# The first head's values' product made to wait for both heads' copies, in the causal attentions and the MLA of a two-block transformer

## The chip, the cores and the metric

The kernel runs on one core of a Trainium2 chip. The metric is the device time of one execution in microseconds (us). Before the change it is 3457.11 us, the median of three runs (3451.3 to 3459.18).

## The reference

Two layers of a hybrid block (a causal attention with forget gates called fox, a sparse attention called nsa, and an MLP) are followed by two layers of a second block (MLA with gated linear attention, then grouped attention, each with a mixture of 16 experts). All is float32, for 512 tokens of width 1024. The change touches the attentions below. With 512 tokens the selection of nsa keeps every block and its window covers every earlier token, so its selected and window branches are plain causal attentions as well.

```python
# fox: 8 heads of 64; nsa's selected and window branches: 8 heads of 64 over 2 key heads
s = jnp.einsum('bhqd,bhkd->bhqk', qi, k) * scale
s = s + ci[..., :, None] - c[..., None, :]            # fox alone
s = jnp.where(kpos[None, :] <= qpos[:, None], s, -jnp.inf)
p = jax.nn.softmax(s, axis=-1)
o = jnp.einsum('bhqk,bhkd->bhqd', p, v)
# MLA: 8 heads, no mask
s = (jnp.einsum('bqhd,bkhd->bhqk', qn, k_nope)
     + jnp.einsum('bqhd,bkd->bhqk', qp, k_pe)) * scale
pr = jax.nn.softmax(s, axis=-1)
o = jnp.einsum('bhqk,bkhd->bqhd', pr, v)
```

## The kernel before

Tokens are held feature-major: 128 features on the partitions, 512 tokens along the free axis. A large product is split in three (`mm3`, L234 to L236): the high part of the weights by the high and the low part of the input, and the low part of the weights by the high part, each a 128x512 product. The weights are split by a cast on ScalarE (L225) and a subtraction (L228).

The causal attentions take two heads at a time. `causal_scores` (L605 to L612) makes for one head four query blocks of 128, with 128, 256, 384 and 512 keys: products into a buffer `s`, a row maximum on VectorE (L610), an exponential on ScalarE (L612). `causal_pv` (L617 to L639) then scales both heads' rows (L288, called from it), and for each key block k of four:

- the probabilities of head 0 are transposed on TensorE into a buffer `pt` (L629, 4 - k transpositions), and VectorE copies them to `PT` (L635);
- the same for head 1, copied by ScalarE (L633);
- one product for each head (L638) multiplies the values `V[h][k]` (128 keys by 64 columns) by `PT[h]` (128 keys by 512, 384, 256 or 128 queries) and adds it to `o`. Head 0's result stands on partitions 0 to 63 of `o`, head 1's on 64 to 127, so each product uses 64 of the 128 columns of TensorE's array.

There are two buffers `pt`, four `PT` and two `s`. `causal_pv` is called 12 times in a layer: four times by fox and eight by nsa (two key heads, two branches, two pairs of heads), so 24 times, with 192 value products.

MLA calls `full_pair` (L997 to L1036) four times. It works on 256 queries at a time, transposes two key blocks at once for each head (L1024), copies head 0 on VectorE (L1030) and head 1 on ScalarE (L1028), and makes four value products of 128x256 (L1035): head 0 and 1 of one key block, then of the next. That is 16 groups of four.

A scheduler sets the order of instructions on every engine when the program is built: it runs a simulated timeline and gives each engine an instruction that its simulation holds to be ready. So products of other work (the projections of the next heads in fox, the merge of fox's output in nsa, handed in piece by piece by generators) stand on TensorE between an attention's steps. Each engine then runs its instructions in that order, and waits where an operand isn't there. No order written by hand holds in these stages; the mixtures of experts have one (`weave`, `keep_order`). In the expert products (L1725) two experts share the array in the same way, 64 columns each, and are written alternately.

Of the kernel before, what the change touches and what calls it, by code (L numbers as in the profile page):

```python
# [147 lines left out]
class K:  # L148
# [303 lines left out]
    def fox(self, l, at, pp, w, XH, XL, v, cneg, B, comp):  # L452
# [3 lines left out]
        def project(pr):  # L456
            if pr % 2 == 0:
                ws[0] = [self.wcols(w, c + 128 * pr) for c in (0, 512)]
            wq, wk = [x[:, :, (pr % 2) * 128:(pr % 2) * 128 + 128] for x in ws[0]]
            Q = self.q_stack(at, pp, wq, XH, XL, None)  # L460
            zk = self.k_proj(at, pp, wk, XH, XL)
            KH = at.tile([128, 2, T], F32R, name="KH", bufs=2)
            KL = at.tile([128, T], F32R, name="KL", bufs=2)
            for h in range(2):
                own = slice(64 * h, 64 * h + 64)
                oth = slice(64 - 64 * h, 128 - 64 * h)
                nc.scalar.copy(KH[own, h], zk[own])
                nc.scalar.copy(KH[oth, h], zk[own])
                nc.vector.tensor_sub(KL[own], zk[own], KH[own, h])
            parts[pr] = Q, KH, KL  # L470
# [25 lines left out]
        for pr in range(4):  # L496
            attend(pr)
            if pr < 2:
                project(pr + 2)

    def put_split(self, B, k, ps):
        self.nc.scalar.copy(B[0][k], ps)
        self.nc.vector.tensor_sub(B[1][k], ps, B[0][k])
# [113 lines left out]
    def causal_pv(self, at, pp, o, P, cf, V, first, last):  # L617

        nc, C = self.nc, self.C
        for h in range(2):  # L620
            for i in range(4):
                self.scale_rows(P[h][0][i], cf[h][:, i:i + 1])
        for k in range(4):
            n = 512 - 128 * k
            PT = []
            for h in range(2):
                ps = pp.tile([128, T], F32, name="pt", tag="t")
                for i in range(k, 4):
                    nc.tensor.transpose(ps[:, (i - k) * 128:(i - k + 1) * 128],  # L629
                                        P[h][0][i][:, k * 128:(k + 1) * 128], C["ident"])  # L630
                pt = at.tile([128, T], F32, name="PT", bufs=4)
                if h:
                    nc.scalar.copy(pt[:, :n], ps[:, :n])  # L633
                else:
                    nc.vector.tensor_copy(pt[:, :n], ps[:, :n])  # L635
                PT.append(pt)
            for h in range(2):
                nc.tensor.matmul(o[64 * h:64 * h + 64, 128 * k:], V[h][k], PT[h][:, :n],  # L638
                                 start=first and k == 0, stop=last and k == 3)  # L639

    def nsa(self, l, p, at, pp, w, XH, XL, gate, gcmp, B, KC, VC, fill):
        nc, tc, I, C, rB = self.nc, self.tc, self.ins, self.C, self.rB
# [354 lines left out]
    def full_pair(self, at, pp, o, passes, V):  # L997

        nc, C = self.nc, self.C
        for half in range(2):  # L1000
            P = []
            for h in range(2):
                p_ = at.tile([128, 2, T], F32, name="P", bufs=3)
                sums = at.tile([128, 2], F32, name="sums", bufs=4)
                mx = at.tile([128, 2], F32, name="mx", bufs=4)
                for i in range(2):
                    qs = slice(256 * half + 128 * i, 256 * half + 128 * i + 128)
                    s = pp.tile([128, T], F32, name="s", tag="s")
                    for j, (q, k) in enumerate(passes[h]):
                        nc.tensor.matmul(s, q[:, qs], k, start=j == 0, stop=j == len(passes[h]) - 1)  # L1010
                    nc.vector.tensor_reduce(mx[:, i:i + 1], s, axis=X, op=OP.max, negate=True)
                    nc.scalar.activation(p_[:, i], s, AF.Exp, bias=mx[:, i:i + 1], accum_out=sums[:, i:i + 1])
                nc.vector.reciprocal(sums, sums)
                for i in range(2):
                    self.scale_rows(p_[:, i], sums[:, i:i + 1])
                P.append(p_)
            for kp in range(2):
                PT = []
                for h in range(2):
                    ps = pp.tile([128, 2, 2, 128], F32, name="pt", tag="t")  # L1020
                    for kk in range(2):
                        for i in range(2):
                            k = 2 * kp + kk
                            nc.tensor.transpose(ps[:, kk, i], P[h][:, i, k * 128:(k + 1) * 128], C["ident"])  # L1024
                    pt = at.tile([128, 2, 256], F32, name="PT", bufs=4)
                    pv = ps.rearrange("p k i q -> p k (i q)")
                    if h:
                        nc.scalar.copy(pt, pv)  # L1028
                    else:
                        nc.vector.tensor_copy(pt, pv)  # L1030
                    PT.append(pt)
                for kk in range(2):
                    k = 2 * kp + kk
                    for h in range(2):
                        nc.tensor.matmul(o[64 * h:64 * h + 64, 256 * half:256 * half + 256], V[h][k], PT[h][:, kk],  # L1035
                                         start=k == 0, stop=k == 3)  # L1036

    def weave(self, plan, **chains):

# [1007 lines left out]
```

## Time and profile before

| | |
|---|---|
| median of three runs | 3457.11 us |
| the profiled execution's own time | 3446.95 us |
| its span | 3445.2 us |
| TensorE busy (PE) | 3255.6 us, 94% of the span |
| VectorE (DVE), ScalarE (ACT), GpSimd (POOL) busy | 1553.8, 1051.8, 581.3 us |
| mean granted TensorE clock | 0.978 of full speed |

The profile is one execution. PE is TensorE's matmuls, PEld its weight loads. A matmul of full float32 operands (L638, L1035, L1725) appears as two records, a transposition and an `mm3` product as one, so "x2" in a row of L638 is one value product. The end of a matmul is modelled and lies after the moment at which the next may start; what an instruction costs is read from the start of one to the start of the next.

### The profile page before, as it was taken

The numbers are of one execution on the slowest core, as the hardware profiler recorded it, in microseconds if no ns is written. First come the engines' busy times: TensorE is split into PE (matmuls) and PEld (weight loads), VectorE is DVE, ScalarE is ACT, GpSimd is POOL, SyncE is SP. The second block draws the span as 40 slices with busy tenths as digits, with TensorE's granted clock in tenths as the row PEclk, the third lists the DMA queues.
The fourth block names the chain that finished last, engine by engine and source line by source line (L and its number), as shares of the span: only waits on it lengthen the run. The fifth ranks groups of instructions, "written<-read, shape, count | busy, mean of one in ns | idle before, by whom it ended". The sixth has DMA issues, their size and how long they took to land. (4 is left out here: it accounts for less than half of the span.)

```text
span 3445.2 us, 37016 instructions
## 1 busy us (share of the span) xinstructions
PE 3255.6 (94%) x14746; PEld 2111.6 (61%) x14746; DVE 1553.8 (45%) x2435; ACT 1051.8 (31%) x1856; POOL 581.3 (17%) x437
## 2 busy tenths in 40 slices
PE   8999999999999999999998889999998889999997
PEld 5666678888766666888875676434345547444343
DVE  6555464334655545444458755122124666211214
ACT  3333333223344333322246423111113443111011
POOL 2012121001101111200121224000002552200001
PEclk9999999999999999999999989999999999999998
DMA  5101132224310111233321115999994113999997
GB/s 186 50 25 50 49 99 86 94 92 136 98 49 25 49 49 63 96 98 98 98 71 39 50 60 205 421 421 396 420 421 178 37 38 122 372 421 395 421 421 296
DMA packets 223724, 585.07 MB, mean 170 GB/s; under 512 B 17600, under 2 KB 160320, under 8 KB 173376
## 3 DMA queue, kind: packets, MB, share of 16 engines
q1 hardware_dynamic: 223120, 581.92, 44.6%
q8 instruction: 116, 1.90, 0.2%
q10 hardware_dynamic: 432, 0.79, 0.1%
q14 instruction: 56, 0.46, 0.0%
HBM read 580.57 MB, written 2.10 MB: 169 GB/s over the span
## 5 line engine op out<-in xcount | busy, mean ns | idle before, releaser
L225 ACT CAST whi<-w 128x1024 fp32r<-128x1024 f32 (+1 forms) x312 | 311.1, 1003 | 709.7 <-PE mm L235 501.6
L1725 PE MATMUL a<-w,xg 128*64 128x512 f32 x2048 | 477.6, 596 | 50.4 <-DMA w<-in_w_dram 50.4
L234 PE MATMUL mm<-h,whi 128*128 128x512 f32 x1056 | 416.3, 394 | 4.8 <-ACT whi L225 4.1
L236 PE MATMUL mm<-h,wlo 128*128 128x512 f32 x1056 | 414.3, 393 | 0.4 <-POOL wlo L228 0.3
L235 PE MATMUL mm<-l,whi 128*128 128x512 f32 x1056 | 412.2, 391 | 0.0
L228 DVE TENSOR_TENSOR wlo<-w,whi 128x1024 fp32r<-128x1024 f32 (+1 forms) x235 | 301.6, 1286 | 213.5 <-ACT whi L225 212.8
L1725 PEld LDWEIGHTS a<-w,xg 128*64 128x64 f32 x2048 | 155.1, 137 | 356.2 <-issue 249.5
L228 POOL TENSOR_TENSOR wlo<-w,whi 128x1024 fp32r<-128x1024 f32 x77 | 171.8, 2235 | 565.2 <-ACT whi L225 541.0
L234 PEld LDWEIGHTS mm<-h,whi 128*128 128x128 f32 x1056 | 198.7, 188 | 48.8 <-ACT whi L225 5.3
L236 PEld LDWEIGHTS mm<-h,wlo 128*128 128x128 f32 x1056 | 198.7, 188 | 45.7 <-DVE wlo L228 0.8
L235 PEld LDWEIGHTS mm<-l,whi 128*128 128x128 f32 x1056 | 198.7, 188 | 44.8 <-issue 0.7
L1725 PE MATMUL y<-w,hT 128*64 128x512 f32 x1024 | 224.7, 594 | 0.0
L1818 DVE SCALAR_TENSOR_TENSOR th<-th,a 128x512 f32<-128x512 f32 x32 | 22.0, 687 | 327.6 <-ACT th L1817 327.6
L610 DVE TENSOR_REDUCE mx<-s 128x1 f32<-128x128 f32 x192 | 93.4, 489 | 153.6 <-PE s L609 152.8
L1725 PEld LDWEIGHTS y<-w,hT 128*64 128x64 f32 x1024 | 72.0, 137 | 140.2 <-issue 138.1
L956 POOL TENSOR_TENSOR u<-u 128x512 f32<-128x512 f32 x64 | 66.6, 1040 | 521.4 <-ACT E L955 275.5
L612 ACT ACTIVATE P<-s,mx 128x128 f32<-128x128 f32 x192 | 101.1, 528 | 166.3 <-DVE mx L610 153.7
L1793 POOL TENSOR_TENSOR og<-OH,aff 128x512 f32<-128x512 f32 x16 | 16.8, 1048 | 716.5 <-DVE oT L1836 700.0
L1817 ACT ACTIVATE th<-a 128x512 f32<-128x512 f32 x32 | 19.1, 597 | 341.6 <-PE a L1725 341.6
L1857 DVE SCALAR_TENSOR_TENSOR yl<-y,gate,yh 128x512 fp32r<-128x512 f32 x32 | 24.0, 751 | 208.9 <-ACT yh L1856 208.9
L967 DVE TENSOR_TENSOR y<-mm,r 128x512 f32<-128x512 f32 x64 | 44.2, 691 | 160.7 <-PE mm L236 160.7
L629 PEld LDWEIGHTS pt<-c_ident,P 128*128 128x128 f32 x480 | 54.4, 143 | 76.1 <-issue 64.8
(614 smaller groups left out, 6326.5 us busy)
## 6 DMA issues: line engine op xcount, KB each, us to landing
w<-in_w_dram SPq DMA_DIRECT2D x384, 1024.0 KB, 12.9
w<-in_w_in_dram SPq DMA_DIRECT2D x32, 1024.0 KB, 5.2
w<-in_w_up_dram SPq DMA_DIRECT2D x32, 1024.0 KB, 5.4
w<-in_w_down_dram SPq DMA_DIRECT2D x32, 1024.0 KB, 5.1
w<-in_w_out_dram SPq DMA_DIRECT2D x8, 1024.0 KB, 5.1
w<-in_w_o_dram SPq DMA_DIRECT2D x8, 1024.0 KB, 4.7
w<-in_ple_gate_w_dram SPq DMA_DIRECT2D x16, 512.0 KB, 9.4
w<-in_w_in_even_dram SPq DMA_DIRECT2D x7, 1024.0 KB, 5.6
```

What stands on the lines that cost most here:

```text
L225: nc.scalar.copy(h, view)
L228: e.tensor_sub(l, view, h)
L234: mm(ps, wh, xh, start=first, stop=False)
L235: mm(ps, wh, xl, start=False, stop=False)
L236: mm(ps, wl, xh, start=False, stop=last)
L610: nc.vector.tensor_reduce(mx[:, i:i + 1], s[:, :n], axis=X, op=OP.max, negate=True)
L612: nc.scalar.activation(pv, s[:, :n], AF.Exp, bias=mx[:, i:i + 1], accum_out=sums[:, i:i + 1])
L629: nc.tensor.transpose(ps[:, (i - k) * 128:(i - k + 1) * 128], P[h][0][i][:, k * 128:(k + 1) * 128], C["ident"])
L956: nc.gpsimd.tensor_mul(u, u, u)
L967: nc.vector.tensor_mul(y, ps, r2)
L1725: nc.tensor.matmul(ps[64 * a:64 * a + 64], lhs(a, 4 * kc + k), cw[a][:, k], start=kc == 0 and k == 0, stop=kc == 1 and k == 3)
L1857: nc.vector.scalar_tensor_tensor(yl, y, gate, yh, op0=OP.mult, op1=OP.subtract)
```

## The change

The first head's value product gets one more dependency: it waits for the copy of the second head's transposed probabilities (on ScalarE), which the second head's product waits for anyway. It adds no instruction and takes none away.

```diff
+    def follow(self, i, done):
+
+        self.tc.add_manual_dep(i.ins, done.ins.name, mybir.DependencyInfo(mybir.DependencyClass.Sync, mybir.DependencyReason.DATA),
+                               reason="pair")
...
                 if h:
-                    nc.scalar.copy(pt[:, :n], ps[:, :n])
+                    done = nc.scalar.copy(pt[:, :n], ps[:, :n])
                 else:
                     nc.vector.tensor_copy(pt[:, :n], ps[:, :n])
                 PT.append(pt)
             for h in range(2):
-                nc.tensor.matmul(o[64 * h:64 * h + 64, 128 * k:], V[h][k], PT[h][:, :n],
-                                 start=first and k == 0, stop=last and k == 3)
+                i = nc.tensor.matmul(o[64 * h:64 * h + 64, 128 * k:], V[h][k], PT[h][:, :n],
+                                     start=first and k == 0, stop=last and k == 3)
+                if h == 0:
+                    self.follow(i, done)
...
                     if h:
-                        nc.scalar.copy(pt, pv)
+                        done = nc.scalar.copy(pt, pv)
...
                     for h in range(2):
-                        nc.tensor.matmul(o[64 * h:64 * h + 64, 256 * half:256 * half + 256], V[h][k], PT[h][:, kk],
-                                         start=k == 0, stop=k == 3)
+                        i = nc.tensor.matmul(o[64 * h:64 * h + 64, 256 * half:256 * half + 256], V[h][k], PT[h][:, kk],
+                                             start=k == 0, stop=k == 3)
+                        if h == 0:
+                            self.follow(i, done)
```

The scheduler makes another order of it. Lines after the new function are 5 to 9 higher in the changed kernel (L629 is L634, L638 is L643, L1024 is L1031, L1035 is L1042). Here is TensorE in nsa's last attention of the first layer, from its last score products on; `pt` is the buffer of transposed probabilities, `o` the output, `l_1436` the values, `nK` and `Q` keys and queries, `mm` the first product of the next stage. First the order before:

```order
L609 MATMUL s<-c_causal,identb 128x128
L638 MATMUL o<-PT,l_1436 64x128
L629 MATMUL pt<-c_ident,P 128x128 x2
L638 MATMUL o<-PT,l_1436 64x512
L629 MATMUL pt<-c_ident,P 128x128 x10
L638 MATMUL o<-PT,l_1436 64x512
L638 MATMUL o<-PT,l_1436 64x384
L629 MATMUL pt<-c_ident,P 128x128 x2
L638 MATMUL o<-PT,l_1436 64x384
L629 MATMUL pt<-c_ident,P 128x128 x2
L638 MATMUL o<-PT,l_1436 64x256
L629 MATMUL pt<-c_ident,P 128x128
```

And the same place in the changed kernel:

```order
L614 MATMUL s<-c_causal,identb 128x128
L634 MATMUL pt<-c_ident,P 128x128 x12
L643 MATMUL o<-PT,l_1436 64x512 x2
L634 MATMUL pt<-c_ident,P 128x128 x2
L643 MATMUL o<-PT,l_1436 64x384 x2
L634 MATMUL pt<-c_ident,P 128x128 x3
L643 MATMUL o<-PT,l_1436 64x256 x2
L634 MATMUL pt<-c_ident,P 128x128
L643 MATMUL o<-PT,l_1436 64x128 x2
L234 MATMUL mm<-h_100,whi 128x512
```

Before, the two products of a size stand apart, with transpositions between them. In the changed order they stand side by side; so do all 96 pairs of the causal attentions.

TensorE in MLA, where `vm` are the values, `K01h` and `K10h` keys and `qn` the projection of the next pair of heads; the order before:

```order
L1024 MATMUL pt<-c_ident,P 128x128 x8
L1010 MATMUL s<-K01h,h_2535 128x512
L1010 MATMUL s<-K01l,h_2535 128x512
L1010 MATMUL s<-K01h,l_2537 128x512
L1035 MATMUL o<-PT,vm 64x256 x3
L1024 MATMUL pt<-c_ident,P 128x128 x4
L1035 MATMUL o<-PT,vm 64x256
```

And in the changed kernel:

```order
L1031 MATMUL pt<-c_ident,P 128x128 x8
L1017 MATMUL s<-K01h,h_2535 128x512
L1017 MATMUL s<-K01l,h_2535 128x512
L1017 MATMUL s<-K01h,l_2537 128x512
L1042 MATMUL o<-PT,vm 64x256 x4
L1031 MATMUL pt<-c_ident,P 128x128 x4
```

Before, the first product of a group stands alone and three follow later, in 12 of the 16 groups. In the changed order all 16 groups stand as four.

## Rows read from the trace of the kernel before

**Rows 1.** The page: busy time by engine.
```profile
PE 3255.6 (94%) x14746; PEld 2111.6 (61%) x14746; DVE 1553.8 (45%) x2435; ACT 1051.8 (31%) x1856; POOL 581.3 (17%) x437
```

**Rows 2.** Windows: PE, PEld, DVE, ACT, POOL busy, clock, DMA; attentions, then MLA.
```profile
119.00:435.00 316.00, 314.79 (x1396) 197.14 (x1395) 167.40 (x360) 122.49 (x296) 48.15 (x26) 0.99 0.14 44
926.00:1268.00 342.00, 340.56 (x1514) 222.56 (x1514) 185.74 (x365) 130.74 (x292) 53.68 (x30) 0.98 0.16 50
1268.00:1330.00 62.00, 57.29 (x229) 31.18 (x228) 28.98 (x69) 22.25 (x59) 0.00 (x0) 0.92 0.05 18
1825.00:1925.00 100.00, 93.57 (x458) 59.37 (x459) 73.26 (x138) 57.56 (x121) 7.87 (x10) 0.99 0.05 13
```

**Rows 3.** Waits of PE, 926 to 1268 us: total, times, longest.
```profile
PE vcp L835 <- DVE mixed L833: 0.8, 1, 0.8
```

**Rows 4.** Windows of L638 alone: PE busy, PEld busy, clock, DMA.
```profile
80.00:600.00 520.00, 69.06 (x192) 17.52 (x192) 0.99 0.19 58
900.00:1330.00 430.00, 72.95 (x192) 18.08 (x192) 0.97 0.15 47
```

**Rows 5.** Windows of L1035 alone, MLA.
```profile
1820.00:1930.00 110.00, 25.92 (x128) 10.25 (x128) 0.97 0.08 21
```

**Rows 6.** Timeline of PE in nsa, first layer: start, us, instructions.
```profile
249.10 0.39 PE L235 MATMUL my<-l,whi 128*128 128x512 f32 x1
249.33 0.40 PE L236 MATMUL my<-h,wlo 128*128 128x512 f32 x1
249.66 1.07 PE L638 MATMUL o<-PT,h 128*64 128x512 f32 x2
250.66 0.55 PE L629 MATMUL pt<-c_ident,P 128*128 128x128 f32 x3
251.14 0.86 PE L638 MATMUL o<-PT,h 128*64 128x384 f32 x2
251.93 0.44 PE L629 MATMUL pt<-c_ident,P 128*128 128x128 f32 x2
```

**Rows 7.** Timeline of PE, first layer's last attentions.
```profile
423.79 1.07 PE L638 MATMUL o<-PT,l 128*64 128x512 f32 x4
424.79 0.44 PE L629 MATMUL pt<-c_ident,P 128*128 128x128 f32 x2
...
427.39 0.65 PE L638 MATMUL o<-PT,l 128*64 128x256 f32 x2
427.96 0.33 PE L629 MATMUL pt<-c_ident,P 128*128 128x128 f32 x1
...
429.06 0.43 PE L638 MATMUL o<-PT,l 128*64 128x128 f32 x2
429.42 0.44 PE L605 MATMUL s<-nK,Q 128*128 128x384 f32 x1
```

**Rows 8.** Timeline of PE in MLA.
```profile
1848.08 1.08 PE L1035 MATMUL o<-PT,vm 128*64 128x256 f32 x6
1849.09 0.66 PE L1024 MATMUL pt<-c_ident,P 128*128 128x128 f32 x4
1849.67 0.65 PE L1035 MATMUL o<-PT,vm 128*64 128x256 f32 x2
```

**Rows 9.** Timeline of PE, second layer's last attentions; idle time before and releaser in brackets.
```profile
1292.53 0.93 PE L629 MATMUL pt<-c_ident,P 128*128 128x128 f32 x7
1294.19 1.07 PE L638 MATMUL o<-PT,l 128*64 128x512 f32 x2 [0.73 <-ACT PT L633]
...
1306.97 1.97 PE L638 MATMUL o<-PT,l 128*64 128x512 f32 x2 [1.26 <-DVE PT L635]
...
1317.16 0.43 PE L638 MATMUL o<-PT,l 128*64 128x128 f32 x2 [0.33 <-ACT PT L633]
```

**Rows 10.** Page, costliest groups: busy us, mean ns, then idle before.
```profile
L225 ACT CAST whi<-w 128x1024 fp32r<-128x1024 f32 (+1 forms) x312 | 311.1, 1003 | 709.7 <-PE mm L235 501.6
```

**Rows 11.** Windows: sum over six stretches at half clock, 220 to 1324 us.
```profile
sum 27.20, PE 26.41 PEld 14.67 DVE 13.43 ACT 6.72 POOL 0.00; mean PE 4.40 PEld 2.45 DVE 2.24 ACT 1.12 POOL 0.00
```

## The prediction

> **What bounds the kernel now.** I read the page first. TensorE is busy 94% of the span, the next engine 45% [rows 1]. An average can hide a stage, so the windows of the stages that the change touches come next: the reader should see TensorE busy 314.79 of 316 us in the first layer's attentions and 340.56 of 342 us in the second's, with VectorE at 167 and 186 us and ScalarE at 122 and 131 us [rows 2]. The list of waits agrees: between 926 and 1268 us the longest one of TensorE is 0.8 us [rows 3]. So in both attentions the end is set by how long TensorE's own instructions take, and by nothing else. Less so in the last 62 us of the second layer's (57.29 us busy) and in MLA (93.57 of 100 us) [rows 2]: the other work that fills TensorE's gaps has run out there, and latencies begin to count.
>
> Then I read the timeline for what one value product costs, from its start to the next start. A 512-query product that stands alone takes 1.00 us (249.66 to 250.66), one of 384 takes 0.79 (251.14 to 251.93) [rows 6], of 256 0.57 and of 128 0.36 [rows 7]. Each also delays what comes ahead of it: products of 128x512 follow each other at 0.23 us (249.10 to 249.33), but the value product starts 0.33 us after the last of them [rows 6]. I put this entry at 0.10 us for every run of value products.
>
> The row on which everything turns is one where two products of different heads happen to stand side by side. Head 1's 512 queries and the next key block's 384 of head 0 run together in 1.00 us (423.79 to 424.79, four records) [rows 7], which is the price of the 512 alone. In MLA three products of 256, of heads 1, 0 and 1, take 1.01 us (1848.08 to 1849.09) [rows 8]: two of head 1 after one another, at about 0.43 each with the 0.15 at the end, and head 0's inside that time. So two value products on opposite halves of the array run at once when nothing stands between them.
>
> **The change, part by part.** It adds one wait to 96 + 32 products and no instruction. Its effect is the order: the wait makes the first product ready when the second is, and the scheduler then places them together. Before, 172 of the 192 value products of the causal attentions stand alone: 40 of 128, 48 of 256, 42 of 384 and 42 of 512 queries. The other 20 stand in ten runs of two, six of them 512 with 384 and four 128 with 128. After, all stand in 96 pairs, 24 of each size.
>
> TensorE's time before, worked out: 40 x 0.36 + 48 x 0.57 + 42 x 0.79 + 42 x 1.00 = 117.0 us, and the ten runs 6 x 1.00 + 4 x 0.37 = 7.5, and 182 entries at 0.10 = 18.2; 142.7 us in all. The trace has these products busy for 69.06 + 72.95 = 142.0 us [rows 4], so the prices hold. After: a pair costs what one costs, 24 x (1.00 + 0.79 + 0.57 + 0.36) = 65.3, and 96 entries 9.6; 74.9 us. The difference is 67.8 us.
>
> MLA before: 12 single products at 0.57, 12 runs of three and 4 of four at 1.01 each, 28 entries: 6.8 + 16.2 + 2.8 = 25.8 us, where the trace has 25.92 [rows 5]. After: 16 runs of four at 1.01 and 16 entries, 17.8 us. The difference is 8.0 us. Together TensorE has 75.8 us less to do.
>
> What takes some of it back is the wait. A pair must now stand behind its second head's copy, and in program order whatever TensorE has queued behind the pair waits too (transpositions of the next key block, score products, the `mm3` stream), and with those the maxima and exponentials. Where other products stand between the last transposition and the pair, they hide the copy: in the changed order that is so for 73 of the 96 pairs, most with ten or more products of 0.23 us. For the other 23 pairs nothing stands there: 16 are in the last three calls of either layer, 7 elsewhere. In MLA it is 6 of the 16 groups. The trace has the price of that: a product of 512 directly behind its transpositions waited 0.73 us for ScalarE's copy, and one of 128 waited 0.33 us [rows 9]. The worst row, 1.26 us [rows 9], lies in a stretch at half clock. I take 0.73 for each, since it is the undisturbed one of the widest copy: 23 x 0.73 = 16.8 us and 6 x 0.73 = 4.4 us. The bounds of this term: nothing if the scheduler's gaps hide all of it as they do now in the first window, and 128 - 16 = 112 waits (one for each pair, and for each MLA group) of 0.73 = 82 us if none is hidden.
>
> The sum: 75.8 - 21.2 = 54.6, say 55 us. Nothing else is late after that as far as the windows show: VectorE would be at 167 of some 288 us. The mixtures of experts, which come after MLA, start that much earlier with an unchanged order of transfers, so the gain reaches the end. The profiled execution would go from 3446.95 to 3392 us. The median shown lies 10 us above that execution, so I forecast 3402 us.
>
> A rule of the Trainium skill speaks against all this. The row first: with two products on opposite column halves the second cost nothing, weight load included [rows 7]. "TensorE: Matmul & The Clock Gate", section "The mechanism" in Part 3, says that a weight load overlaps a running product only where the two use different row groups; our pairs use all 128 rows and differ in columns alone. By that rule the pair would run one after the other, which is the second rival below; by the row it doesn't. The same page's section "Measured speedup vs the span model" gives 2.38 times for three column tiles, 0.79 of the ideal; taken over to two tiles that is an estimate of 1.59 times, and the sum by it would be about 31 us.
>
> **Rivals.** (1) Half the gain. The scheduler's simulation placed the other work; if it holds a pair to cost two, TensorE reaches each next step sooner than planned, and waits for maxima, exponentials and copies appear where rows 3 show hardly any. For it: the row 1.26 us shows what a late copy costs. Against: a call of the woven stretches loses some 2.8 of about 26 us (12 calls in 316 us), while VectorE has half its time free [rows 2]. If another 0.27 us is lost at each of 96 pairs (26 us), the gain is 29 us: 3428.
>
> (2) No overlap, the pairs run one after the other. Then only entries and the 0.15 us at a run's end are saved: 182 + 28 - 96 - 16 = 98 runs fewer at 0.25 = 24.5 us, less 21.2 of waits: 3 us, and the time is 3454. Against it stand the four-record and six-record rows [rows 7, 8].
>
> (3) Slower: ScalarE takes its instructions in order, and the copy that now holds both products can stand behind a weight cast of 1.00 us [rows 10]. Then the pair waits up to 0.73 + 1.00 = 1.7 us at the head of TensorE's queue. The change breaks even where the mean wait over the 112 pairs and groups reaches 75.8 / 112 = 0.68 us; at 0.85 us it loses 95 and the time is 3476. For it: ScalarE casts for the same `mm3` stream that hides the copy. Against: most pairs have over 2 us of products ahead of them.
>
> (4) The clock. Six stretches, 27.2 us in all, ran at 0.50 of full speed (1.2 GHz) between 220 and 1324 us [rows 11]; before them TensorE had run transpositions and single value products, or had waited. That is some 13.6 us lost now. Either none or twice as many would move the forecast by about 13 us, within its own range.
>
> **How the numbers follow.** Forecast (gain of 38 to 76 us, the upper end being all of TensorE's saving with no wait): 0.79. Rival 1 (10 to 38): 0.12. Rival 2: 0.04. Rival 3: 0.05. For 8 in 10 the range runs from 3380 (76 us of gain) to 3432, just past rival 1. A change under 0.2%, 7 us, can't be told from none. Faster: the forecast and rival 1, 0.91. Same: rival 2 and a little of rival 3, 0.05. Slower: the rest of rival 3, 0.04.
>
> **What would show it.** The value products' busy time falls from 142 to about 75 us, and rows of a single size appear with four records and the duration of two. In MLA, runs of eight records take about 1.01 us. Waits of TensorE for `PT` grow to some 20 us, nearly all in the last 60 us of either layer's attentions and in MLA. If the busy time stays above 130 us, pairs don't overlap. If it falls and the time doesn't, the waits say where it went: many waits for ScalarE's copy are rival 3, waits for maxima and exponentials rival 1. It would be wrong altogether if the mixtures started earlier and ended no earlier.

## The result, and the profile after

The changed kernel takes 3410.18 us (median of four runs, 3407.67 to 3416.08) where the kernel before takes 3454.6 us (median of four, 3451.3 to 3459.18): 44 us less, a ratio of 0.9873 with a 95% interval of 0.9854 to 0.9892. The forecast was 3402 us and a gain of 55. The profiled execution took 3407.67 us, 39.3 less than the profiled one of before (3446.95); that one lay further under its median.

The page of the changed kernel, busy time by engine, against [rows 1]: TensorE is busy for 56 us less, the others nearly as long as before.

```profile
PE 3199.4 (94%) x14746; PEld 2111.0 (62%) x14746; DVE 1561.1 (46%) x2435; ACT 1049.1 (31%) x1856; POOL 582.3 (17%) x437
```

Windows of the value products alone in the changed kernel, causal attentions (L643) and MLA (L1042); columns are length, PE busy, PEld busy, clock, DMA share and GB/s:

```profile
80.00:600.00 520.00, 39.42 (x192) 9.89 (x192) 0.98 0.20 62
900.00:1320.00 420.00, 40.54 (x192) 10.08 (x192) 0.95 0.17 52
...
1780.00:1920.00 140.00, 17.34 (x128) 7.75 (x128) 0.98 0.11 34
```

PE's busy time in the causal attentions is the sum of the first two, 80.0 us, from 142.0 [rows 4], and in MLA 17.3 from 25.9 [rows 5]. The timeline of PE in the second layer shows pairs of each size, four records to a row:

```profile
1217.95 0.87 PE L643 MATMUL o<-PT,h 128*64 128x384 f32 x4
1218.75 0.55 PE L634 MATMUL pt<-c_ident,P 128*128 128x128 f32 x3
...
1223.94 0.65 PE L643 MATMUL o<-PT,h 128*64 128x256 f32 x4
1224.52 0.33 PE L634 MATMUL pt<-c_ident,P 128*128 128x128 f32 x1
...
1227.03 0.44 PE L643 MATMUL o<-PT,h 128*64 128x128 f32 x4
1227.40 0.33 PE L610 MATMUL s<-nK,Q 128*128 128x128 f32 x1
...
1232.72 1.08 PE L643 MATMUL o<-PT,h 128*64 128x512 f32 x4
1233.73 0.76 PE L634 MATMUL pt<-c_ident,P 128*128 128x128 f32 x5
```

From start to next start a pair of 512 takes 1.01 us, of 384 0.80, of 256 0.58, of 128 0.37: what one alone took [rows 6, 7], plus 0.01. In MLA eight records take what six took [rows 8], 1.01 us from their start to the next:

```profile
1849.51 1.08 PE L1042 MATMUL o<-PT,vm 128*64 128x256 f32 x8
1850.52 0.50 PE L1017 MATMUL s<-K10h,h 128*128 128x512 f32 x1
```

So the saving on TensorE is there. What took part of it back stands in two other views. The list of PE's waits from 80 to 1330 us (both layers of the first block; what waited, for whom, total, times, longest), first four rows of the changed kernel, then four of the kernel before:

```profile
PE pt L634 <- DVE P L288: 4.5, 2, 2.4
PE o L643 <- ACT PT L638: 3.9, 8, 0.7
PE mm L234 <- ACT whi L225: 3.3, 2, 1.6
PE s L610 <- ACT P L617: 3.1, 6, 0.7
```

```profile
PE o L638 <- DVE PT L635: 2.0, 2, 1.3
PE s L605 <- ACT P L612: 1.5, 3, 0.7
PE o L638 <- ACT PT L633: 1.1, 2, 0.7
PE pt L629 <- DVE P L288: 0.4, 1, 0.4
```

The waits for ScalarE's copy are 3.9 us (1.1 before), for the late scaling 4.5 (0.4 before), for exponentials 3.1 (1.5 before). Those for VectorE's copy, 2.0 us before, are gone. So the value products wait for copies 0.8 us longer than before, and all four kinds together 6.5 us longer. In MLA (1780 to 1930 us) the row for the copy was the first of these before and is the second now:

```profile
PE o L1035 <- ACT PT L1028: 0.7, 1, 0.7
PE o L1042 <- ACT PT L1035: 2.1, 5, 0.7
```

And the windows in which TensorE's clock stood at 0.50, that is 1.2 GHz, in the changed kernel's attentions:

```profile
1242.90:1266.70 23.80, 20.90 (x68) 9.95 (x65) 9.51 (x26) 7.36 (x21) 0.00 (x0) 0.50 0.00 0
396.40:403.20 6.80, 6.07 (x20) 3.22 (x19) 2.07 (x5) 2.09 (x6) 0.00 (x0) 0.50 0.00 1
413.50:416.90 3.40, 3.40 (x10) 0.88 (x10) 0.42 (x1) 0.66 (x2) 0.00 (x0) 0.50 0.00 0
...
sum 57.80, PE 53.67 PEld 28.84 DVE 27.03 ACT 16.95 POOL 0.37; mean PE 8.94 PEld 4.81 DVE 4.50 ACT 2.83 POOL 0.06
```

The first row is the second layer's last attentions, the next two the first layer's. The dots stand for three earlier stretches; the sum of the six is 57.8 us, where the kernel before has 27.2 in its six [rows 11]. In the 7 us ahead of the long one TensorE ran transpositions, score products and value pairs, and no 128x512 `mm3` product. In the kernel before, the second layer's last attentions had a single half-clock stretch, the fifth of the six in [rows 11]:

```profile
1306.20:1313.00 6.80, 6.01 (x16) 2.44 (x16) 2.89 (x9) 1.84 (x4) 0.00 (x0) 0.50 0.00 0
```

Where the two profiled executions stand at the end of each stage (start or end of a product of that stage in the timeline of PE, us):

| | before | after | difference |
|---|---|---|---|
| first layer's attentions end | 441.6 | 420.1 | -21.6 |
| second layer's attentions end | 1317.6 | 1270.3 | -47.3 |
| MLA's first scores | 1833.8 | 1789.9 | -43.9 |
| MLA's values end | 1921.4 | 1872.3 | -49.1 |
| first expert product | 2123.4 | 2080.7 | -42.7 |
| last expert product | 3421.8 | 3382.1 | -39.7 |

The causal attentions gave 47 us and MLA 5; some 13 us were lost again in stages that get no new wait, though the scheduler moved the order in some of them.

### The profile page after: what moved, and what is told of

It is laid out like the page before. It is cut to its first block, busy times and chain, and to the rows that moved or that the text cites. A ratio compares the mean times of both kernels' runs of the same rounds, so it can differ in the third digit from the quotient of the medians.

```text
span 3405.9 us, 37009 instructions
## 1 busy us (share of the span) xinstructions
PE 3199.4 (94%) x14746; PEld 2111.0 (62%) x14746; DVE 1561.1 (46%) x2435; ACT 1049.1 (31%) x1856; POOL 582.3 (17%) x437
## 5 line engine op out<-in xcount | busy, mean ns | idle before, releaser
L236 PE MATMUL mm<-h,wlo 128*128 128x512 f32 x1056 | 415.8, 395 | 0.1
L235 PE MATMUL mm<-l,whi 128*128 128x512 f32 x1056 | 412.5, 391 | 0.0
L236 PEld LDWEIGHTS mm<-h,wlo 128*128 128x128 f32 x1056 | 199.2, 189 | 46.6 <-DVE wlo L228 1.0
L235 PEld LDWEIGHTS mm<-l,whi 128*128 128x128 f32 x1056 | 199.3, 189 | 45.5 <-issue 0.7
L234 PE MATMUL mm<-E,whi 128*128 128x512 f32 x256 | 99.7, 389 | 0.0
```

Of the source, the lines that this page charges most:

```text
L234: mm(ps, wh, xh, start=first, stop=False)
L235: mm(ps, wh, xl, start=False, stop=False)
L236: mm(ps, wl, xh, start=False, stop=last)
```

## The experiments

Theory after the result: two value products on opposite column halves run at once, which is the whole gain; TensorE's clock, which in this kernel fell where transpositions, scores and pairs were all that was left, takes part of it back. The rivals are that the gain comes from the new order, that the waits took the missing part, and that the order behind MLA took it.

**The wait in the causal attentions alone.**

```diff
                         i = nc.tensor.matmul(o[64 * h:64 * h + 64, 256 * half:256 * half + 256], V[h][k], PT[h][:, kk],
                                              start=k == 0, stop=k == 3)
-                        if h == 0:
-                            self.follow(i, done)
```

> The wait stands in the causal attentions alone; MLA is as before, and from the final norm of the first block on TensorE's order is word for word that of the kernel before. Theory: the causal attentions gave 48.6 us of the gain, and MLA's 5.2 us were lost again in the gated linear attention behind it, whose order the MLA change moved. Then this kernel stands within 3 us of the changed one, at 3406 to 3412 us. Rival: MLA's gain is real and the loss behind it was the clock of one execution; then it is 5 us slower than the changed one, 3415 us.

Measured: 3414.44 us, a ratio of 0.9879 (0.9852 to 0.9906). The theory on the order behind MLA falls, but not for the rival's reason alone. In this kernel's profile the attentions end 44.0 us earlier than before and MLA 42.7, and then 13 us are lost all the same, to 29.9 at the last expert product, though TensorE's order there is that of the kernel before. The windows from MLA's end to the first expert product, first of before, then of this kernel (length, PE, PEld, DVE, ACT and POOL busy, clock, DMA share and GB/s, as in all windows of this section):

```profile
1921.00:2123.00 202.00, 172.03 (x948) 145.24 (x947) 132.70 (x219) 79.43 (x140) 66.98 (x49) 0.87 0.23 84
```

```profile
1879.00:2087.00 208.00, 181.09 (x947) 153.63 (x946) 132.99 (x219) 79.09 (x140) 66.97 (x49) 0.84 0.23 81
```

It is 6 us longer, PE's busy time is 9 us longer for the same products, and the clock is 0.84 against 0.87. The half-clock time there is 68 us against 51, and half of the difference, 8.5 us, is more than the 6. So a loss of such a size can come from the clock alone. Much of it belongs to the two executions that were profiled: by the medians 40 of the 44 us arrive (3454.26 to 3414.44), since the profiled execution of before lay 7 us under its median and this one 3 us over.

**The wait in MLA alone** (the converse edit: the two lines of `follow` are taken out of the causal attentions).

> The wait stands in MLA alone. Theory: MLA itself ends 5 us earlier, the gated linear attention takes 6 us more, and the total does not move: 3452 to 3457 us. Rival: the 5 us reach the end, 3449 us.

Measured: 3455.6 us, a ratio of 0.9999 (0.9985 to 1.0014). In its profile the first block's attentions end 1.6 us later than before and MLA's values 3.7 us earlier, so MLA gives 5.3 us, and the total does not move. That is what the theory expected, but since its reason fell with the run above, I leave open whether MLA's 5 us reach the end: the changed kernel is 4 us under the one with the causal wait alone, with intervals that overlap, and the interval of this run (5 us either way) would hold a gain of 5 us as well.

**Pairs side by side, but on the same columns.**

```diff
-                i = nc.tensor.matmul(o[64 * h:64 * h + 64, 128 * k:], V[h][k], PT[h][:, :n],
-                                     start=first and k == 0, stop=last and k == 3)
+                i = nc.tensor.matmul(o[:64, 128 * k:], V[h][k], PT[h][:, :n],
+                                     start=first and k == 0 and h == 0, stop=last and k == 3 and h == 1)
```

> As the changed kernel, but the second head's value products of the causal attentions write the same 64 partitions as the first head's, so both use the same columns of the array (the second half of o is then not the attention's result, and fox's output is copied out in two halves). Theory: the gain is that two products on opposite column halves run at once; without it each pair costs 0.85, 0.64, 0.43 or 0.21 us more, 24 x 2.13 = 51 us, and the time is about 3461 us, value products busy about 130 us. Rival: the gain comes from fewer entries and exits and from the new order; then the time stays near 3410 us and the busy time near 80.

Measured: 3438.48 us, a ratio of 0.9958 (0.9946 to 0.9971): 28 us slower than the changed kernel. The timeline of PE in this kernel, and the windows of all instructions on `PT` (PE busy, PEld busy, the copies on DVE and ACT, then as before):

```profile
246.62 1.93 PE L649 MATMUL o<-PT,h 128*64 128x512 f32 x4
248.48 0.76 PE L640 MATMUL pt<-c_ident,P 128*128 128x128 f32 x5
```

```profile
80.00:600.00 520.00, 65.30 (x192) 22.45 (x192) 23.39 (x48) 20.38 (x48) 0.00 (x0) 0.98 0.18 57
900.00:1320.00 420.00, 63.22 (x192) 21.94 (x192) 23.37 (x48) 20.38 (x48) 0.00 (x0) 0.99 0.16 48
```

A pair of 512 now takes 1.86 us, and all of them 128.5 us, 48.6 more than in the changed kernel and close to the 130 expected. That settles the overlap. The time rose by less than 51 us, and the clock goes a long way to say why: up to the end of the first block's attentions the half-clock stretches add up to 34 us here and to 68 in the changed kernel, a difference worth 17 us. With more work on TensorE the clock stayed up. This kernel is still 16 us faster than the one before, so the overlap in the causal attentions is most of the gain and not all of it: in the profile the attentions end 11 us earlier than before, and MLA's groups stand as in the changed kernel. The waits did not change: 4.2 us for ScalarE's copy, 4.2 for the late scaling and 2.2 for exponentials, against 3.9, 4.5 and 3.1.

**Work held back for the last attentions.** Three of the four gate projections that fill TensorE in nsa wait for the first exponential of the newest attention.

```diff
-        mm(ps, wh, xh, start=first, stop=False)
+        i = mm(ps, wh, xh, start=first, stop=False)
+        if first and self.held is not None:
+            self.follow(i, self.held)
+            self.held = None
...
+            if i == 0:
+                self.begun = e
...
+            if m:
+                self.held = self.begun
             self.proj(ps, wg[:, :, (m % 2) * 128:(m % 2) * 128 + 128], XH, XL, pool=True)
```

In the second cut `i` counts a head's four exponentials, and `e` is the newest of them.

> As the changed kernel, but three of the four gate projections that fill TensorE in nsa (24 products each, some 16 us in all) wait for the first exponential of the newest attention, so that they stand in the last attentions of either layer, where nothing filled TensorE and the clock was at half speed for 23.9 us (second layer). Theory: the last attentions lose time to half clock and to waits for copies and scaling; with work there the half-clock stretch shrinks below 10 us and the kernel is 5 to 12 us faster than the changed one, 3398 to 3405 us. Rival: the last attentions are held by the chain of maxima, exponentials and scalings whatever the clock is; the work only moves, and waits appear where it stood: 3408 to 3413 us.

Measured: 3400.68 us (3397.84 to 3403.19), a ratio of 0.9842 (0.9819 to 0.9865), 9.5 us under the changed kernel's median: the fastest version of the study. The two intervals overlap at their edges (0.9854 to 0.9892 for the changed kernel), but the slowest of these four runs is faster than the fastest of the changed kernel's four (3407.67). The window of the second layer's last 36 us of attentions, first of the changed kernel, then of this one:

```profile
1236.00:1272.00 36.00, 29.76 (x115) 14.41 (x114) 15.06 (x40) 13.03 (x38) 0.00 (x0) 0.67 0.00 1
```

```profile
1230.00:1266.00 36.00, 31.91 (x164) 20.23 (x162) 16.04 (x40) 13.59 (x34) 2.40 (x1) 1.00 0.10 30
```

In the same 36 us TensorE does nearly the same attention work and 60 of the 72 held products (164 records against 115), at full clock. In the first layer it did not work: a half-clock stretch of 17 us stands where the projections were taken away, and that layer ends no earlier than in the changed kernel (20.9 us ahead of before, against 21.6).

**Value products one key block later**, behind the next block's transpositions, to hide the copy.

```diff
+        late = []
         for k in range(4):
...
                 PT.append(pt)
-            for h in range(2):
-                i = nc.tensor.matmul(o[64 * h:64 * h + 64, 128 * k:], V[h][k], PT[h][:, :n],
-                                     start=first and k == 0, stop=last and k == 3)
-                if h == 0:
-                    self.follow(i, done)
+            late.append((k, n, PT, done))
+            for k, n, PT, done in (late if k == 3 else late[:-1]):
+                for h in range(2):
+                    i = nc.tensor.matmul(o[64 * h:64 * h + 64, 128 * k:], V[h][k], PT[h][:, :n],
+                                         start=first and k == 0, stop=last and k == 3)
+                    if h == 0:
+                        self.follow(i, done)
+            late = late[-1:]
```

> As the changed kernel, but in the causal attentions the value products of key block k are written behind the transpositions of block k + 1, so that these hide the second head's copy. Theory (waits): the 3.9 us of waits for ScalarE's copy in the causal attentions go, and some of the 4.5 us for the late scaling; 3 to 6 us faster than the changed kernel's 3410, 3404 to 3407 us. Rival (clock): the waits are only where TensorE has nothing else to do and runs at half clock; taking them away draws the same half-clock stretches elsewhere, and the time stays within 2 us of 3410.

Measured: 3412.14 us, a ratio of 0.9877 (0.9858 to 0.9896); no faster, as the rival said. Value products no longer stand in the list of PE's waits, but in the last attentions of either layer a stretch of 27.3 us runs at half clock (10.2 and 23.8 us in the changed kernel):

```profile
395.30:422.60 27.30, 23.72 (x72) 11.21 (x72) 11.44 (x31) 7.92 (x25) 0.00 (x0) 0.50 0.00 0
1248.60:1275.90 27.30, 23.70 (x72) 11.19 (x72) 11.43 (x31) 7.94 (x25) 0.00 (x0) 0.50 0.00 0
```

**Both together, and the holding alone in another spread** (`self.held = self.begun[(10, 12, 13, 14)[m]]`, with the first exponentials of nsa's 16 heads kept in order).

> The kernel before this one (value products one block later) and the gate projections held back for the last three attentions, one each for four exponentials, so that two of them don't fall together as in the run with three held. Theory (both add): waits and half clock in the last attentions go; 3393 to 3400 us. Rival (one cover is enough): the held work already hides the copies, and the time is that of the run with held work alone, 3400 us, or worse by the later products.

> The changed kernel with the four gate projections held back for four different exponentials of the last attentions, without the later value products. Theory (clock and waits of the last attentions): like the run with three held, or better by the two projections that lay together there: 3395 to 3401 us, half-clock stretches of the second layer's attentions under 25 us. Rival: the gain of the run with three held was the clock of those runs; then 3407 to 3413 us.

Measured: 3418.23 us (0.9897, 0.9879 to 0.9915) and 3406.46 us (0.9860, 0.9840 to 0.9879). The first theory is refuted: the two don't add. The second kernel lies between what the theory and the rival said; its half-clock stretches are 27 us in the second layer (41 in the changed kernel), just over the 25 expected, but 41 in the first (24 in the changed kernel), where some stand at the place the projections had left.

**Products that nobody needs.** In the last three attentions of each layer, one or three 128x512 products go into each buffer ahead of its transpositions. The diff is that of one; the other kernel has `range(3)`, and `idle`, two parts of the stage's input, is handed in for those three attentions alone.

```diff
+                if idle:
+                    for _ in range(1):
+                        nc.tensor.matmul(ps, idle[0][:, :128], idle[1], start=True, stop=True)
                 for i in range(k, 4):
                     nc.tensor.transpose(ps[:, (i - k) * 128:(i - k + 1) * 128],
```

> As the changed kernel, but in the last three causal attentions of each layer one product of 128x512 that nothing uses goes into each buffer of transposed probabilities before its transpositions: 24 a layer, 5.5 us at 0.23 each, 11 us in all. Theory (clock): the half-clock stretches of the last attentions (10.2 us in the first layer, 27.3 in the second) come where TensorE does transpositions, small score products and pairs alone; with a large product among them they shrink to less than half, and with the waits that the products fill the time is 3402 to 3412 us in spite of 11 us more work. Rival: the clock doesn't depend on them; the products only lengthen TensorE's work, 3418 to 3430 us.

> The same with three such products in each place: 72 a layer, 33 us in all. Theory (clock): no half-clock stretch is left in the last attentions, which gives back up to 17 us, and the products hide up to 10 us of waits: 3412 to 3422 us, half of their cost. Rival: 3436 to 3455 us, with half-clock stretches as long as in the changed kernel.

Measured: 3406.95 us (0.9856, 0.9841 to 0.9871) and 3422.19 us (0.9895, 0.9879 to 0.9912). Both times are where the theory had them, the second at its upper end. With one product each the half-clock stretches of the last attentions come to 3.4 us in the first layer and 13.7 in the second, from 10.2 and 23.8 (the 27.3 of the expectation holds a stretch of 3.4 that lies behind the attentions' end). That is half in all; less than half, as the theory wanted, it is in the first layer alone. Eleven microseconds of useless products made the kernel no slower (3407 against 3410), and 33 us cost 12. The windows of the last attentions of both layers with three products each:

```profile
395.00:427.00 32.00, 30.44 (x149) 17.88 (x147) 14.26 (x37) 10.66 (x31) 0.00 (x0) 1.00 0.00 1
1230.00:1280.00 50.00, 49.23 (x241) 29.60 (x240) 23.25 (x61) 17.17 (x50) 0.00 (x0) 1.00 0.00 0
```

The clock is at 1.00 in both. PE's idle time in the attentions fell as well, so the recovered time is clock and filled waits together; the two times alone don't part them.

The kernels' profiles side by side: how much earlier than before the second layer's attentions end, and how long the clock stood at half from the start of the execution to there (us):

| | earlier by | at half clock | earlier, with half of the added half-clock time put back |
|---|---|---|---|
| before | 0 | 34 | 0 |
| changed | 47.3 | 68 | 64 |
| causal alone | 44.0 | 82 | 68 |
| work held back | 53.2 | 58 | 65 |
| one block later | 39.1 | 96 | 70 |
| later and spread | 37.3 | 78 | 60 |
| spread | 45.6 | 68 | 63 |
| one product added | 42.2 | 55 | 52 |
| three products added | 35.1 | 34 | 35 |
| same columns | 11.1 | 34 | 11 |

The first six below the row of before make the same value pairs. Their gains differ by 16 us; with the clock put back they lie within 60 to 70, near the 67.8 us worked out for TensorE, less a few waits. The last three give TensorE some 11, 33 and 51 us more work by the expectations' own sums. With that added to the last column they come to 63, 68 and 62 us, in the same range. So by this estimate all nine kernels lie between 60 and 70 us, and a few us at most are left to the filled waits.

The granted clock that is on record for every execution says the same as the profiled ones: 0.972 to 0.978 for the kernel before, 0.968 to 0.971 for the changed one, 0.966 to 0.968 for the causal wait alone, 0.973 to 0.975 with three products added and 0.973 to 0.978 on the same columns.

The last column is an estimate: it takes TensorE to be busy all through such a stretch, which the first window at 0.50 above (20.90 of 23.80 us) shows to be nearly so.

## Why the prediction came out as it did

**The overlap** was read rightly, and from two rows [rows 7, 8]. A pair costs what one product costs, to 0.01 us; the sum for MLA after (17.8 us) met 17.3. For the causal attentions 74.9 us was predicted and 80.0 measured; the difference lies in the 12 of the 96 pairs that ran at half clock (six of 512 took 1.91 us each instead of 1.01). The prediction let a rule of the Trainium skill stand against it ("TensorE: Matmul & The Clock Gate", Part 3, "The mechanism"): that a weight load overlaps a running product only in other row groups. It took this to mean that pairs would run one after the other. The same section also lets a load go ahead where it targets the background weight buffer, which the prediction left out; no row here names the buffer. With the rule by itself the traces disagree. Weight loads (PEld) run inside products that use all 128 rows, in the `mm3` streams for one: in the kernel before, the load for L236 lies inside the product of L235, from 249.10 to 249.29 us:

```profile
249.10 0.39 PE L235 MATMUL my<-l,whi 128*128 128x512 f32 x1
249.10 0.19 PEld L236 LDWEIGHTS my<-h,wlo 128*128 128x128 f32 x1
```

They do so as well where both products of a pair use the same columns, although that pair takes 1.86 us (246.62 to 248.48 in PE's rows above):

```profile
247.10 0.14 PEld L649 LDWEIGHTS o<-PT,h 128*64 128x64 f32 x1 [0.29 <-issue]
247.53 0.14 PEld L649 LDWEIGHTS o<-PT,h 128*64 128x64 f32 x1 [0.29 <-issue]
```

So hidden weight loads are not what opposite columns add: there the two products themselves run at once. Two products of 512 alone take 2.00 us and their pair 1.01, which is 1.98 times where the prediction's estimate for two tiles had 1.59.

**The entries and exits** were not tested by themselves, but the balance fits: with pairs on the same columns, which save only these, the causal attentions still ended 11 us earlier than before, at the same half-clock time (34 us). By the prediction's 0.25 us, 86 runs fewer are 21.5 us, and some 6 us more of waits take part of that back.

**The waits for the copy** were mis-sized: the term was 21.2 us (29 waits of 0.73 us), and the trace has 3.9 us in the causal attentions, eight times, and 2.1 in MLA, five times. Being without cover in TensorE's order did not mean waiting: one row at 0.73 us in each layer, the others 0.41 or less, and 15 of the 23 pairs none. Nor is all of it new, since the value products had waited 3.1 us for copies before, and 0.7 in MLA; the change added 2.2 us. In their place stand waits that the sum did not have, for scaling and exponentials (7.6 us, from 1.9), which is rival 1 at a small price, as TensorE now reaches the next step ahead of the others.

**The clock** is the term that the sum left out. The prediction's fourth rival named the outcome, "none or twice as many" half-clock stretches, and its price of about 13 us, but it put them as equally open, gave them no chance and kept them within the range. Twice as many came: the change thins out the last attentions, the half-clock time up to their end rises from 34 to 68 us, and up to 17 us of the gain goes there. It was not the chance of one execution, since the recorded clocks of the two kernels' executions don't overlap (0.968 to 0.971 against 0.972 to 0.978), and it went back to 34 us in both kernels that put the most work back on TensorE (pairs on the same columns, three added products). With the trace's sizes the sum is 75.8 less 17 for the clock, 2.2 for the copies and 5.7 for the other waits, some 51 us, and the profile has 52 for the attentions and MLA together. So the forecast of 55 came near the measured 44 partly by luck: the waits for copies were set too high by some 15 to 19 us and the clock at nothing, and the two errors nearly cancel.

**That the gain reaches the end** held within what can be told: by the medians 44 us arrive of the 52 that the attentions and MLA give in the profile. Where the other 8 go stays open, and so does whether MLA's 5 us are among them. The profiled executions lose 9 to 14 us behind MLA or the attentions, in the run with TensorE's order unchanged as well.

**Rivals 2 and 3** are refuted: pairs overlap, and no pair waits for ScalarE's copy longer than 0.73 us, where a copy behind a weight cast would have made it up to 1.7. The three signs named for the profile came: rows of four records at one product's duration, runs of eight in 1.01 us, and a busy time of the value products of 80 us, near the 75. The sign for the waits (some 20 us for `PT`) did not.

## What to carry to other kernels

Two products that use opposite halves of the array's columns can be worth placing side by side, and a wait that makes the first ready no earlier than the second is a cheap way to get a scheduler to do so: look in the trace for a place where it happens by accident, and read its price there. When a change takes work off TensorE, read the granted clock of that stage afterwards. Here some of the gain went to a slower clock where nothing else filled the stage, and bringing other work there gave part of it back, as in the version with work held back (3400.68 us).

## What the runs showed of the hardware that was not expected

Adding 33 us of useless 128x512 products to stages that ran at half clock for 34 us cost 12 us of time, and adding 11 us cost none. Two products on opposite column halves cost 0.01 us more than one, while two on the same half cost 0.86 us more, though weight loads ran inside products in both. Two profiled executions can differ in half-clock time in a stage in which TensorE runs the same instructions in the same order: from MLA's end to the first expert product it was 51 us in the kernel before and 68 in the one with the causal wait alone, and that stage was 6 us longer.
